# First batch's stage: token tables in four pieces beside the channel tiles, the odd weight sums in the other room, the weight work pinned to the outer rows alone

## The chip, the cores and the metric

The kernel runs on one core of one Trainium2 chip. Five engines work side by side, each through its own instructions in a fixed order: TensorE (PE, with its weight loads as PEld), VectorE (DVE), ScalarE (ACT), GpSimd (POOL) and SyncE (SP), which here only issues transfers. They wait for each other through semaphores. The metric is the device time of one execution in microseconds. The kernel before has a median of 2423.64 us over three runs (2421.47 to 2424.58).

## The reference

The kernel computes one encoder layer for two inputs ("batches") of 1024 tokens by 1024 channels, with the same weights, in float32.

```python
def encoder_layer(x, g_pre, w_in, ...):
    xn = rmsnorm(x, g_pre)
    p = xn @ w_in
    fv, fg, hv, hg, mg = jnp.split(p, ...)
    fz = fv.astype(jnp.float32).reshape(B, L, F_GROUPS, F_GROUP_DIM)
    fz = jnp.fft.fftn(fz, axes=(1, 3), norm="ortho").real
    y_f = (fz * jax.nn.silu(fg)) @ w_fourier_out
    ...
    y_h = (z.astype(dt) * jax.nn.silu(hg)) @ w_hyena_out   # z: two long convolutions
    g_f, g_h = jnp.split(jax.nn.sigmoid(mg + b_merge), 2, axis=-1)
    out = (g_f * y_f + g_h * y_h) @ w_out
    return x + rmsnorm(out, g_post)
```

The change lies in the first 65 us, where the first batch is normalised and multiplied with the part of `w_in` that makes `fv`, and where the token half of the Fourier transform begins.

## The kernel before, in words

Every float32 operand of a matrix product is split into a high and a low part (`split`): ACT rounds the source into the high part (line 170), and DVE or POOL subtracts it from the source to get the low part (line 180). A product is then three matrix multiplications (`mm3`): high by high, high by low, low by high.

The first batch's stage is `first_half`. Its eight tiles of 128 tokens are loaded in two groups: four outer row tiles (0, 7, 1, 6) and four inner ones (2, 5, 3, 4). For each group, `scale_rows` takes the mean square of each row (ACT, line 335), the inverse root of it in a chain of eleven small DVE instructions (`rstd`, lines 241 to 252), and multiplies the rows by it (line 342 on DVE, line 340 on ACT).

Then the channels are passed in four pairs of tiles (`kp` from 0 to 3), first with the outer rows (`h` = 0) and then with the inner rows (`h` = 1). This document numbers these eight steps h0.0 to h0.3 and h1.0 to h1.3. Each step does the following in `two_tiles`:

- TensorE transposes two tiles of 128 channels (line 358), and ACT copies each from PSUM into `xg`, multiplied by `g_pre` (line 359). `xg` has two rooms. Two columns at its end are set by a POOL memset when `h` is 0 (line 353) and by an ACT copy when `h` is 1 (line 351).
- SP stores each tile to `d_x` (line 361).
- The Fourier transform over tokens is folded: `eo` takes the sum and the difference of a token and its mirror image. The sum is made on DVE. The difference is made on DVE when `h` is 0 and on POOL when `h` is 1.
- `eo` is split into `eh` (ACT) and `el` (DVE).
- TensorE multiplies: 24 products `pfv` for a pair of channel tiles, of which 16 read `eh` and 8 read `el`. The first 8 in the order read `eh` alone.

`two_weights` prepares the weights for a pair of channel tiles: the load of `wfv` (line 384, two rooms), the even sums `wes` and odd differences `wos` on DVE, the casts to `we` and `wo` on ACT, and the low parts: `we` on DVE, `wo` on POOL from the second pair on. `wos` has two rooms, `qp0` and `qp1`, taken in turn. The room `qp0` is also that of the scratch `sq` of `hidden(0)`, the sine layer of the filter network, which runs at the same time.

The program is written in loops, and a scheduler in the compiler puts the instructions of every engine in order by its own forecast of their times. `tc.issue_after(i)` tells it to put those instructions of the enclosed part that run on the engine of instruction `i` behind `i`. In the kernel before, `two_weights` and `two_tiles` of all steps but the first stand behind `self.scaled`, the last row scaling on DVE, which from h0.1 on is that of the inner rows. An engine never reorders at run time.

The token tables `seq` (2 MB), the channel tables `chan` and `chx`, the sign table `alt` and the vector `vec` are loaded in `phase_fourier` once `first_half` has been written down: `vec` by SP, the others by POOL. For `seq` and `chan` a tiny POOL copy from `self.rs` (line 631) holds the load back until the inner rows' inverse roots exist. The tables `th`, `wsh` and `bm`, which the main phase uses, are loaded by SP (line 998).

After the stage, `fourier_half` takes the first half's token transform (`pse`, `pso` from `seq`), the channel transform (`pP`, `pQ` from `chan`), and meanwhile the second half's weights and products run. The second batch follows in another form (`norm`, `xtile`), then the main phase.

Of the kernel before, what the change touches and what calls it, by code (L numbers as in the profile page):

```python
# [16 lines left out]
P = 128  # L17
# [143 lines left out]
class K:  # L161
# [167 lines left out]
    def scale_rows(self, h, px, ss, rs):  # L329
# [7 lines left out]
        for j, m in enumerate(self.ROWS[h]):  # L337
            s = rs[:, 4 * h + j:4 * h + j + 1]
            if j % 2 or (h and j):
                nc.scalar.mul(self.xs[m], self.xs[m], s)  # L340
            else:
                self.scaled = nc.vector.tensor_scalar(self.xs[m], self.xs[m], s, None, op0=MUL)

    def two_tiles(self, h, kp, px, fo):
# [4 lines left out]
        xg = px.tile([P, 2, 514], F32, tag="xg", name=f"xg0_{h}{kp}", bufs=2)  # L349
        if h:  # L350
            nc.scalar.copy(xg[:, :, 512:513], fo["r6"][:, ks].unsqueeze(2))
        else:
            nc.gpsimd.memset(xg[:, :, 512:514], 0.0)
# [17 lines left out]
        self.sub("pool" if h else "dve", eo[:, :, 1], fw, bw)  # L371
# [18 lines left out]
    def first_half(self, pw, W, fo, px, pf):  # L390
# [9 lines left out]
        made = None  # L400
        for h in range(2):
# [187 lines left out]
    def phase_fourier(self):  # L589
        tc, nc, a = self.tc, self.nc, self.a  # L590
        with ExitStack() as es:
# [18 lines left out]
            for t in [fo[n] for n in ("x5", "x5t", "xx", "px")] + fo["ex"]:  # L610
                if len(t.shape) > 2:
                    t = t.rearrange("p a b -> p (a b)")
                nc.vector.tensor_scalar(t, self.ident[:, 0:1].to_broadcast(list(t.shape)), 0.0, None, op0=MUL)
            for b in range(NB):
# [3 lines left out]
                if b == 0:  # L618
                    self.hidden(0, px, pf)
                    W = self.open_weights(pw)  # L620
                    made, begun = self.first_half(pw, W, fo, px, pf)
# [5 lines left out]
                for half in ((0, 1), (1, 0))[b]:  # L627
                    if b + half == 0:
                        nc.sync.dma_start(self.vec, a["c_vec"])
                        for t in ("seq", "chan"):  # L630
                            nc.gpsimd.tensor_copy(fo[t][:, 0, 0:1], self.rs[:, 7:8])
                        nc.gpsimd.dma_start(fo["seq"], a["c_seq"])
# [341 lines left out]
    def phase_main(self, nct=8, nb=NB, nf=16):  # L974
        tc, nc, a = self.tc, self.nc, self.a
        with ExitStack() as es:
# [20 lines left out]
            for t, n in ((self.th, "c_th"), (self.wsh, "w_short"), (self.bm, "b_merge")):  # L997
                nc.sync.dma_start(t, a[n])
# [583 lines left out]
```

## Time and profile before

| | us |
|---|---|
| median of three runs | 2423.64 |
| lowest, highest run | 2421.47, 2424.58 |
| time of the profiled execution | 2421.76 |
| its span | 2420.0 |
| PE busy in the span | 2370.0 |
| DVE busy | 1902.7 |
| ACT busy | 1072.7 |
| POOL busy | 511.5 |

The time of the profiled execution is 1.8 us more than its span, and 1.9 us under the median. In the views below, a window row gives for each engine the busy time in that stretch and in brackets the number of instructions, then the granted TensorE clock (1.00 is full), the busy share of the transfer engines and the GB/s. A row of waits names the waiting engine and tile, what ended the wait, the sum, how often, and the longest. A timeline row gives start, duration, engine, line, operation, tiles, and in square brackets the idle time before it with its releaser.

### The profile page before, as it was taken

The page shows a single profiled execution, that of the slowest core. Times are in us where ns is not written, and L with a number is a line of the kernel's source. Part 1 is how long each engine was busy: PE and PEld are TensorE (multiplying, and loading weights), DVE is VectorE, ACT ScalarE, POOL GpSimd, SP SyncE. Part 2 cuts the span into 40 slices and gives each one's busy share as a digit, 9 for nine tenths or more (in the row PEclk, how much of TensorE's full clock was granted, in tenths as well). Part 3 has the DMA queues.
Part 4 walks back from the last instruction along what each step waited for, and adds up shares of the span by engine and source line. Part 5 has one row for each costly group of instructions (what it writes and reads, how often), then busy time and mean ns, then how long its engine had stood idle before and what let it go on. Part 6 is the DMA issues. An engine that isn't in the chain of part 4 may idle for free.

```text
span 2420.0 us, 36378 instructions
## 1 busy us (share of the span) xinstructions
PE 2370.0 (98%) x13000; PEld 2057.5 (85%) x13000; DVE 1902.7 (79%) x3388; ACT 1072.7 (44%) x2037; POOL 511.5 (21%) x521
## 2 busy tenths in 40 slices
PE   5999999999999999999999999999999999999998
PEld 4988888888888888888888888888888888888886
DVE  7776898889749999999889999866555456665677
ACT  6546676767533333333222222332444444444443
POOL 3341222222243334441000000112100111122111
PEclk9999999999999999999999999999999999999999
DMA  7546655555565555546444444445444667786443
GB/s 273 167 147 209 201 182 169 167 176 173 159 204 179 174 168 186 163 153 213 138 132 144 135 138 141 132 138 179 164 162 156 205 211 258 242 269 220 160 158 131
DMA packets 228480, 428.33 MB, mean 177 GB/s; under 512 B 23734, under 2 KB 89592, under 8 KB 227914
## 3 DMA queue, kind: packets, MB, share of 16 engines
q1 hardware_dynamic: 201069, 333.11, 42.9%
q0 software_dynamic: 27008, 92.86, 11.3%
q8 instruction: 102, 1.67, 0.3%
q14 instruction: 80, 0.66, 0.1%
q10 hardware_dynamic: 221, 0.04, 0.0%
HBM read 290.12 MB, written 135.79 MB: 176 GB/s over the span
## 4 chain that ended last, share of the span: by engine, by line
PE 53%; DMA 1%; DVE 1%; issue 1%; ACT 0%; POOL 0%; DVEq 0%; ACTq 0%; POOLq 0%
PE pin L193 18%; PE pg L193 7%; PE pyh L193 7%; PE po L193 6%; PE pyf L193 6%; PE pT L193 4%; PE pX L193 4%; DMA wr<-in_w_fo 1%; PE tph L892 1%; DMA wh<-d_w 0%; DVE b L180 0%; DVE wl L180 0%; DVE t L180 0%; DVE o L176 0%; ACT wh L170 0%
## 5 line engine op out<-in xcount | busy, mean ns | idle before, releaser
L193 PE MATMUL pin<-xh,wh 128*128 128x512 f32 x1472 | 576.6, 392 | 2.4 <-DMA wh<-d_w 1.2
L193 PE MATMUL pin<-xh,wl 128*128 128x512 f32 x1472 | 577.0, 392 | 1.5 <-DMA wr<-in_w_in 1.5
L193 PE MATMUL pin<-xl,wh 128*128 128x512 f32 x1472 | 576.4, 392 | 1.2 <-DVE xl L180 1.2
L180 POOL TENSOR_TENSOR wl<-wr,wh 128x512 fp32r<-128x512 f32 x136 | 255.7, 1880 | 1121.6 <-ACT wh L170 1080.4
L193 PEld LDWEIGHTS pin<-xh,wh 128*128 128x128 f32 x1472 | 277.1, 188 | 55.5 <-DMA wh<-d_w 2.1
L193 PEld LDWEIGHTS pin<-xl,wh 128*128 128x128 f32 x1472 | 277.2, 188 | 53.8 <-DVE xl L180 2.0
L193 PEld LDWEIGHTS pin<-xh,wl 128*128 128x128 f32 x1472 | 277.2, 188 | 53.4 <-POOL wl L180 2.2
L170 ACT CAST wh<-wr 128x512 fp32r<-128x512 f32 x264 | 163.4, 619 | 330.8 <-PE pin L193 102.0
L193 PE MATMUL pX<-bh,cfwd 128*128 128x256 f32 x768 | 162.0, 289 | 0.0
L180 DVE TENSOR_TENSOR wl<-wr,wh 128x512 fp32r<-128x512 f32 x128 | 87.9, 687 | 93.5 <-ACT wh L170 93.4
L180 DVE TENSOR_TENSOR t<-pX,k 128x1024 f32<-128x1024 f32 x128 | 155.4, 1214 | 5.5 <-PE pX L193 3.8
L193 PE MATMUL pyf<-sf,wh 128*128 128x512 f32 x512 | 157.8, 389 | 0.0
L193 PE MATMUL pyh<-sh,wh 128*128 128x512 f32 x512 | 157.4, 389 | 0.0
L193 PE MATMUL pT<-cinv,yh 128*128 128x256 f32 x768 | 145.6, 285 | 0.0
L170 ACT CAST bh<-b 128x512 fp32r<-128x512 f32 x144 | 88.7, 619 | 111.5 <-DVE b L180 76.0
L193 PEld LDWEIGHTS pX<-bh,cfwd 128*128 128x128 f32 x768 | 126.7, 191 | 2.7 <-DVE t L180 0.4
L193 PEld LDWEIGHTS pT<-cinv,yh 128*128 128x128 f32 x768 | 123.2, 190 | 6.6
L170 ACT CAST yh<-y 128x512 fp32r<-128x512 f32 x96 | 59.5, 619 | 138.0 <-DVE y L180 135.5
L193 PEld LDWEIGHTS pyf<-sf,wh 128*128 128x128 f32 x512 | 96.2, 188 | 19.9
L193 PEld LDWEIGHTS pyh<-sh,wh 128*128 128x128 f32 x512 | 96.1, 188 | 19.9
L193 PE MATMUL pT<-cinv,yl 128*128 128x256 f32 x384 | 109.5, 285 | 0.1
L193 PE MATMUL pX<-bl,cfwd 128*128 128x256 f32 x384 | 108.9, 283 | 0.6 <-DVE bl L180 0.6
(372 smaller groups left out, 5318.1 us busy)
## 6 DMA issues: line engine op xcount, KB each, us to landing
k<-d_k SPq DMA_DIRECT2D x128, 512.0 KB, 4.2
wr<-in_w_in SPq DMA_DIRECT2D x136, 256.0 KB, 3.2
d_g<-gt SPq DMA_DIRECT2D x124, 256.0 KB, 2.6
d_k<-kt SPq DMA_DIRECT2D x128, 128.0 KB, 2.2
d_k<-kt SPq DMA_DIRECT2D x64, 256.0 KB, 2.5
wr<-in_w_fo POOLq DMA_DIRECT2D x64, 256.0 KB, 4.1
g<-d_g SPq DMA_DIRECT2D x64, 256.0 KB, 4.2
wr<-in_w_ho POOLq DMA_DIRECT2D x64, 256.0 KB, 3.8
```

The source lines that it names most:

```text
L170: self.rounded = nc.scalar.copy(h, src)
L180: return e.tensor_tensor(out, a, b, op=op)
L193: return self.nc.tensor.matmul(out, lhsT, rhs, start=start, stop=stop, skip_group_check=shared)
L892: nc.tensor.transpose(tp[:, q * P:(q + 1) * P], eo[:, e, q], self.ident)
```

## The change

- `scale_rows`: of the inner rows, the third is scaled on DVE and no longer on ACT. `self.scaled` becomes that instruction.
- `two_tiles`: the end columns are always set by a POOL memset (one column when `h` is 1, beside the ACT copy), which becomes `self.cleared`. The difference in `eo` is always on DVE.
- `two_weights`: the odd differences `wos` take the rooms in the other order, so that the first pair takes `qp1` and not the room of the sine layer's scratch.
- `first_half`: `two_weights` of the second to fourth pair stands behind the outer rows' last DVE scaling alone; `two_tiles` still stands behind the inner rows' one. After each step, POOL issues a part of the tables behind that step's memset: the four pieces of `seq` (even high, even low, odd high, odd low) with steps h0.2 to h1.1, `alt` with h1.0, `chan` and `vec` with h1.2, and `chx`, `th`, `wsh` and `bm` with h1.3.
- The loads in `phase_fourier` and `phase_main` that this replaces, and the two tiny POOL copies, are gone.

```diff
@@ scale_rows
-            if j % 2 or (h and j):
+            if j % 2:
                 nc.scalar.mul(self.xs[m], self.xs[m], s)
             else:
                 self.scaled = nc.vector.tensor_scalar(self.xs[m], self.xs[m], s, None, op0=MUL)
@@ two_tiles
+        self.cleared = nc.gpsimd.memset(xg[:, :, 512 + h:514], 0.0)
         if h:
             nc.scalar.copy(xg[:, :, 512:513], fo["r6"][:, ks].unsqueeze(2))
-        else:
-            nc.gpsimd.memset(xg[:, :, 512:514], 0.0)
...
         self.add("dve", eo[:, :, 0], fw, bw)
-        self.sub("pool" if h else "dve", eo[:, :, 1], fw, bw)
+        self.sub("dve", eo[:, :, 1], fw, bw)
@@ two_weights
-        wo = pf.tile([P, 2, 256], F32, tag=f"qp{kp % 2}", name="wos", bufs=1)
+        wo = pf.tile([P, 2, 256], F32, tag=f"qp{1 - kp % 2}", name="wos", bufs=1)
@@ first_half
-        made = None
+        scaled, made = self.scaled, None
...
             for kp in range(4):
+                if h == 0 and kp:
+                    with tc.issue_after(scaled.ins):
+                        self.two_weights(px, pw, pf, W, kp)
                 with tc.issue_after(self.scaled.ins) if h + kp else ExitStack():
-                    if h == 0 and kp:
-                        self.two_weights(px, pw, pf, W, kp)
                     self.two_tiles(h, kp, px, fo)
+
+                with tc.issue_after(self.cleared.ins):
+                    for t, src in later[4 * h + kp]:
+                        self.nc.gpsimd.dma_start(t, src)
@@ phase_fourier
+            n = 4 * 258
+            seq = [(fo["seq"][:, h, n * e:n * e + n], a["c_seq"][:, h, n * e:n * e + n])
+                   for e in range(2) for h in range(2)]
+            later = [[], [], seq[0:1], seq[1:2], seq[2:3] + [(fo["alt"], a["c_alt"])], seq[3:4],
+                     [(fo["chan"], a["c_chan"]), (self.vec, a["c_vec"])],
+                     [(fo["chx"].rearrange("p a b c -> p (a b c)"), a["c_chx"]), (self.th, a["c_th"]),
+                      (self.wsh, a["w_short"]), (self.bm, a["b_merge"])]]
...
-                    if b + half == 0:
-                        nc.sync.dma_start(self.vec, a["c_vec"])
-                        for t in ("seq", "chan"):
-                            nc.gpsimd.tensor_copy(fo[t][:, 0, 0:1], self.rs[:, 7:8])
-                        nc.gpsimd.dma_start(fo["seq"], a["c_seq"])
-                        nc.gpsimd.dma_start(fo["alt"], a["c_alt"])
-                        nc.gpsimd.dma_start(fo["chan"], a["c_chan"])
-                        nc.gpsimd.dma_start(fo["chx"].rearrange("p a b c -> p (a b c)"), a["c_chx"])
-                    elif b + half != 2:
+                    if b + half not in (0, 2):
@@ phase_main
-            for t, n in ((self.th, "c_th"), (self.wsh, "w_short"), (self.bm, "b_merge")):
-                nc.sync.dma_start(t, a[n])
```

More of the change, by code (lines that the diff above doesn't have):

```diff
@@ L388, in two_weights, with first_half @@
             self.split(*[p[:, 2 * kp:2 * kp + 2] for p in W[i]], r, "pool" if kp and i else "dve", "act")
-    def first_half(self, pw, W, fo, px, pf):
+    def first_half(self, pw, W, fo, px, pf, later):
         tc = self.tc
@@ L620, in phase_fourier @@
                     W = self.open_weights(pw)
-                    made, begun = self.first_half(pw, W, fo, px, pf)
+                    made, begun = self.first_half(pw, W, fo, px, pf, later)
                 else:
```

## The prediction

> **What bounds the kernel now.** I read the page's head, the busy time by stage, TensorE's waits in the changed stage, and then the stage's timeline.
>
> ```profile
> PE 2370.0 (98%) x13000; PEld 2057.5 (85%) x13000; DVE 1902.7 (79%) x3388; ACT 1072.7 (44%) x2037; POOL 511.5 (21%) x521
> 17.90:25.70 7.80, 6.41 (x24) 4.29 (x24) 3.48 (x14) 7.25 (x14) 0.20 (x2) 1.00 0.39 136
> 25.70:39.00 13.30, 11.07 (x73) 10.54 (x72) 11.49 (x18) 11.20 (x19) 5.31 (x7) 0.87 0.93 310
> 39.00:50.00 11.00, 7.26 (x56) 6.48 (x55) 10.28 (x15) 8.12 (x17) 6.68 (x3) 1.00 0.78 263
> 50.00:60.00 10.00, 7.99 (x64) 7.58 (x63) 9.76 (x11) 3.92 (x9) 6.12 (x5) 1.00 0.71 249
> 60.00:70.00 10.00, 10.00 (x86) 9.87 (x85) 3.65 (x11) 3.45 (x10) 3.34 (x5) 1.00 0.04 15
> ```
>
> From 60 us TensorE is full: 86 matmuls in 10 us, 0.116 us each. From 25.7 to 60 it does 193 in 34.3 us, and these would take 22.4 us at that pace. So some 12 us are lost in this stage, and DVE is the busy engine there (9.76 of the last 10 us). Then DVE is nearly idle (3.65 of 10) and TensorE still works: it has piled up work. What ends its waits:
>
> ```profile
> PE pfv L193 <- ACT eh L170: 4.1, 2, 2.2
> PE pfv L193 <- POOL wo L180: 1.8, 2, 1.4
> PE pfv L193 <- DVE el L180: 1.6, 1, 1.6
> ```
>
> ACT's `eh` is itself held up (the waits of ACT), and the groups of DVE and POOL from 18 us show by whom:
>
> ```profile
> ACT eh L170 <- POOL eo L180: 4.7, 3, 2.7
> L180 DVE TENSOR_TENSOR el<-eo,eh 128x1024 fp32r<-128x1024 f32 x8 | 12.4, 1546 | 0.9 <-ACT eh L170 0.8
> L180 DVE TENSOR_TENSOR eo<-xg 128x512 f32<-128x512 f32 x12 | 9.4, 812 | 0.4 <-ACT xg L359 0.2
> L180 DVE TENSOR_TENSOR we<-wes,we 128x520 fp32r<-128x520 f32 x3 | 3.4, 1134 | 0.0
> L180 DVE TENSOR_TENSOR wer<-wfv 128x260 f32<-128x260 f32 x2 | 2.3, 1184 | 0.0
> L180 POOL TENSOR_TENSOR eo<-xg 128x512 f32<-128x512 f32 x4 | 9.5, 2364 | 8.5 <-ACT xg L359 4.7 <-DVE el L180 3.8
> L180 POOL TENSOR_TENSOR wo<-wos,wo 128x512 fp32r<-128x512 f32 x3 | 5.1, 1700 | 0.8 <-ACT wo L170 0.8
> L180 POOL TENSOR_TENSOR wor<-wfv 128x256 f32<-128x256 f32 x2 | 1.9, 960 | 0.0
> ```
>
> POOL needs 2.36 us for a difference for which DVE, alone, needs 0.62 (four in 2.49, below). And DVE slows down beside POOL: the rows below show `el` at 1.21 us alone and 2.10 beside POOL's `wo`. Against the undisturbed 1.22 (`el`), 0.62 (`eo`), 0.69 (`we`) and 0.42 (`wer`), the four DVE groups hold 2.6 + 2.0 + 1.3 + 1.4 = 7.3 us too much, beside 16.5 us of POOL subtraction.
>
> ```profile
> 13.75 0.61 ACT L170 CAST we<-wes 128x520 fp32r<-128x520 f32 x1
> 13.87 0.76 DVE L180 TENSOR_TENSOR wos<-wfv 128x256 f32<-128x256 f32 x2 [1.07 <-ACT hd L270]
> 14.62 0.69 DVE L180 TENSOR_TENSOR we<-wes,we 128x520 fp32r<-128x520 f32 x1
> 22.28 0.17 DVE L241 TENSOR_SCALAR rs_m<-ss 128x4 f32<-128x4 f32 x1 [3.77 <-ACT sq L335]
> 24.61 1.04 ACT L170 CAST eh<-eo 128x1024 fp32r<-128x1024 f32 x1
> 27.02 0.76 DVE L342 TENSOR_SCALAR x<-x,rs 128x1024 f32<-128x1024 f32 x1
> 27.04 3.23 ACT L340 ACTIVATE x<-x,rs 128x1024 f32<-128x1024 f32 x3
> 27.70 0.42 DVE L180 TENSOR_TENSOR wes<-wfv 128x260 f32<-128x260 f32 x1
> 29.05 2.49 DVE L180 TENSOR_TENSOR eo<-xg 128x512 f32<-128x512 f32 x4
> 31.21 1.04 ACT L170 CAST eh<-eo 128x1024 fp32r<-128x1024 f32 x1
> 31.39 1.91 POOL L180 TENSOR_TENSOR wo<-wos,wo 128x512 fp32r<-128x512 f32 x1 [0.85 <-ACT wo L170]
> 32.28 2.10 DVE L180 TENSOR_TENSOR el<-eo,eh 128x1024 fp32r<-128x1024 f32 x1
> 32.30 0.74 PE L193 MATMUL pfv<-we,eh 128*128 128x260 f32 x4 [2.17 <-ACT eh L170]
> 45.53 1.77 DVE L180 TENSOR_TENSOR eo<-xg 128x512 f32<-128x512 f32 x1 [0.16 <-ACT xg L359]
> 57.89 1.21 DVE L180 TENSOR_TENSOR el<-eo,eh 128x1024 fp32r<-128x1024 f32 x1
> 67.57 0.64 PE L193 MATMUL pse<-seq,ee 128*128 128x258 f32 x4
> ```
>
> The last `el` is done at 59.1, and TensorE reaches the end of the first half's products at 67.57. That instant is what the sum below moves. From there on the kernel is TensorE's, which is busy for 98% of the span.
>
> **The change part by part.** Orders are those of the two built programs, durations those of the rows above.
>
> *Odd sums in the other room.* `wos` of the first pair no longer waits for ACT's `hd` (1.07 us). But the chain of the outer rows has `we` in it, which needs ACT's cast (to 14.36 us). So `we` comes at 14.40 and not at 14.62: 0.2 us gained.
>
> *Weight work pinned to the outer rows.* The sums and differences of the second pair, and one more, now stand in DVE's idle 3.77 us before 22.28. But the rest of the third pair's work goes in ahead of the inner rows' scaling: two `wos`, two `wes` (0.34 from start to start) and two `we` (0.69), together 2.7 us. And ACT gets two casts ahead of the transposed tiles of h0.1, which puts `eh` of h0.0 (24.61) back by 0.4 to 1.2 us; that is covered, since TensorE waits later anyway. So the scaling starts at 27.02 + 2.7 - 0.2 = 29.5. With one more scaling on DVE (two, 1.45 us), `eo` of h0.1 starts at 31.0 and not 29.05, is done at 32.2, `eh` at 33.3, and TensorE goes on at 33.3 and not at 32.30. This is a loss. Its upper end: POOL's `wo` of the second and the third pair now run beside `eo` and `el` of h0.0, which by the rows cost DVE 0.9 us (2.10 against 1.21) and 1.15 (1.77 against 0.62). TensorE then goes on at 35.4. ACT's third scaling going to DVE saves ACT 1.07 and costs DVE 0.72; both are in these numbers.
>
> *Differences on DVE.* Four more on DVE cost 4 x 0.62 = 2.5 us and take 9.5 us off POOL. POOL keeps 7.0 us of subtraction, so of the 7.3 us lost by slowing some 7.3 x 7.0 / 16.5 = 3.1 stay, and 4.2 come back. DVE's account: -4.2 + 2.5 + 0.7 (scaling) - 2.0 (six small sums, 0.34 each, in idle time) = -3.0. The last `el` is done at 56.1, or, if the 4.2 do not come back, at 60.3. Behind it stand 16 products, 1.9 us: 62.2 at the latest. This does not set the end, since TensorE's own work does:
>
> *TensorE.* The order has 222 matmuls from the products of h0.1 to the end of the half. They take 222 x 0.116 = 25.8 us. To this come the slower clock behind the wait, 5 x (0.15 + 0.19) = 1.7 us by the rows below, and short waits for PSUM, 0.5 to 1.1 us. From 33.3: 61.3. From 35.4 with the longer waits: 64.0. Against 67.57 that is 6.3 or 3.6 us less; both ends rest on the same two rows, and I take the middle, **5.0 us**. The gain comes mostly from products that no longer pile up: the `wo` products of the inner rows are in step with the others in the new order, while before they came behind the last `el`.
>
> ```profile
> 30.00:35.00 5.00, 2.77 (x16) 2.43 (x15) 4.73 (x6) 4.60 (x10) 2.01 (x2) 0.85 0.92 371
> 35.00:40.00 5.00, 4.12 (x28) 3.88 (x26) 3.50 (x7) 2.40 (x5) 1.54 (x1) 0.81 0.99 319
> 135.00:140.00 5.00, 3.75 (x21) 3.73 (x21) 5.00 (x7) 3.56 (x7) 3.46 (x3) 0.66 0.52 209
> 120.00:140.00 20.00, 15.48 (x115) 14.55 (x114) 19.50 (x30) 14.90 (x25) 11.29 (x11) 0.91 0.84 298
> seq<-in_c_seq POOLq DMA_DIRECT2D x1, 2064.0 KB, 9.7
> 27.76 0.53 POOL L632 DMA_DIRECT2D seq<-in_c_seq  x1
> wfv<-in_w_fv SPq DMA_DIRECT2D x20, 260.0 KB, 3.4
> ```
>
> *Tables in pieces, on POOL.* Costed at nothing. TensorE first reads `seq` behind 160 of the 222 matmuls, about 53 us; its two pieces are issued with h0.2 and h0.3, before 35 us, and the whole table took 9.7 us to land. The odd pieces are needed after 65 us and issued by 46. SP loses four small issues. POOL gains seven issues (0.53 each, 3.7 us) and four tiny memsets, and loses two tiny copies. Behind them on POOL stand the `wo` subtractions and the memsets, and each memset holds an `xg`, so ACT's copy. The tightest is h1.1's: behind the fourth pair's `wo` and a `wor` it comes about 39.5, and its transposes about 42. If that 2.5 us of cover is gone, ACT and then `eo` of h1.1 are late by what is missing; TensorE has h0.3 to do meanwhile.
>
> *Behind the stage.* The second half's weights start when TensorE has read the first half's for the last time, so they move with it. All later work is the same; its order is shuffled up to about the 3,700th matmul. I cost that at nothing, between the bounds of the rivals.
>
> The sum: -5.0 us. The profiled execution took 2421.76, so it would be 2416.8; this execution lies 1.9 under the median of the runs, and against the median of 2423.64 it is **2418.6**.
>
> **The rivals.**
>
> *The inner rows come later still, and the clock drops (0.12).* The third pair's first `wos` is ahead of `eo` of h0.0, and its weights can be asked for only when a room is free, about 19 us; with 3.4 us to land they are there when DVE comes (22.6). If they are 1 us late, all behind is: products from 36.4, after a wait of 6 us. The longer wait can cost more clock: the row from 135 us shows 0.66, 1.7 us lost in 5. Then 36.4 + 25.8 + 1.7 + 1.7 + 1.1 = 66.7, and only 0.9 us are left: 2422.7. [...]
>
> *The shuffled order behind the stage wins (0.22).* TensorE's idle time from 120 to 140 us is 4.5 us, with 1.8 of clock (0.09 x 20). If the new order avoids most of it, it is some 5 us more: 2413.6. For it: nothing but that DVE is full there (19.50 of 20) and could start earlier. Against it: the same tiles in the same form.
>
> *The shuffled order loses: slower (0.18).* The place is the second batch's tiles. There TensorE's order has transposes and first-batch products in turn, and a transpose that stands ahead of its transfer, or of DVE, holds ready products behind it. One more such stretch costs 4.5 + 1.8 = 6.3 us. The gain of 5.0 is used up by it; the kernel is slower by more than 0.2% when 9.9 us are lost. Two more stretches, 12.6 us, give 2431.2. Against it: the tiles, transfers and products are the same, and whatever the stage gains gives DVE an earlier start there.
>
> *The change does not do what it says* would be: POOL is still the one that `eh` waits for, through its memsets. It is in the first rival's range.
>
> **How the numbers follow.** A measurement of this kernel tells about 0.2%, 4.8 us, from no change. The forecast has 0.48, its own range 2415 to 2422, with 0.27 of it below 2418.8. Faster: 0.27 + 0.22 = 0.49. Within: 0.21 + 0.12 = 0.33. Slower: 0.18. The range from 2411 to 2428 takes in the forecast, the first two rivals with their spread (2413.6 less 2.6; 2422.7) and the mild end of the third; what it leaves out is about 0.17 above and 0.03 below.
>
> **What would show it.** Step by step in the changed kernel: `we` of the first pair about 14.4; the products of h0.1 from 33.3 to 35.4, so a longer wait there than 2.17; no POOL `eo` row, and no wait of `eh` for POOL; fewer DVE microseconds in `el`, `eo` and `we` by about 4, except for four more `eo`; the first-half products ending between 61 and 64; no wait for `seq` or `chan`. Wrong would be: products of h0.1 after 36.5, a wait of ACT for a memset, `el` still at over 1.5 us on average, or TensorE's idle time from 75 to 280 us more than 5 us above that of before.

## The result, and the profile after

| | before | changed |
|---|---|---|
| median of six runs on one chip, us | 2424.11 (2421.47 to 2427.22) | 2412.94 (2410.63 to 2416.65) |
| ratio, 95% interval | | 0.9955 (0.9942 to 0.9968) |
| the same kernel in a later comparison, us | 2422.77 | 2414.54 (2412.45 to 2417.91) |
| ratio, 95% interval | | 0.9968 (0.9955 to 0.9980) |
| time of the profiled execution, us | 2421.76 | 2412.46 |
| its span, us | 2420.0 | 2410.7 |

The kernel became faster by 0.45% (0.32% in the second comparison). That is 11 and 8 us; 5.0 were forecast. The time lies in the predicted range (2411 to 2428), under the likeliest case's own (2415 to 2422), and near the rival "the shuffled order behind the stage wins" (2413.6). It lies in the range because the range was made to take in that rival.

The rows by stage, for the same stretches as before:

```profile
17.90:25.70 7.80, 6.07 (x24) 4.44 (x25) 5.57 (x15) 7.42 (x15) 2.29 (x4) 1.00 0.60 190
25.70:39.00 13.30, 9.86 (x70) 9.38 (x68) 13.16 (x25) 10.64 (x19) 6.07 (x7) 1.00 0.75 218
39.00:50.00 11.00, 9.75 (x83) 9.54 (x82) 9.24 (x15) 6.95 (x15) 6.03 (x8) 1.00 0.94 287
50.00:60.00 10.00, 10.00 (x87) 9.87 (x86) 5.06 (x8) 4.30 (x9) 2.24 (x5) 1.00 0.79 239
120.00:140.00 20.00, 17.38 (x134) 16.93 (x133) 19.97 (x33) 12.16 (x20) 13.64 (x11) 0.91 0.69 246
```

From 39 to 60 us TensorE now does 170 matmuls; before it did 120. It is full from 46 us on, not from 60. From 25.7 to 39 it does no more than before (70 against 73), because the products of h0.1 wait longer. TensorE's waits in the stage, and the groups of DVE and POOL from 18 to 60 us:

```profile
PE pfv L193 <- ACT eh L170: 4.2, 2, 2.9
PE tpx L357 <- ACT xg L358: 1.5, 3, 0.5
PE pfv L193 <- DVE el L180: 0.5, 1, 0.5
```

```profile
L180 DVE TENSOR_TENSOR el<-eo,eh 128x1024 fp32r<-128x1024 f32 x8 | 10.5, 1328 | 3.5 <-ACT eh L170 3.4
L180 DVE TENSOR_TENSOR eo<-xg 128x512 f32<-128x512 f32 x16 | 10.2, 684 | 0.3 <-ACT xg L358 0.3
L180 DVE TENSOR_TENSOR we<-wes,we 128x520 fp32r<-128x520 f32 x3 | 2.1, 689 | 0.0
L180 POOL TENSOR_TENSOR wo<-wos,wo 128x512 fp32r<-128x512 f32 x3 | 8.5, 2822 | 3.9 <-ACT wo L170 3.9
```

The wait for POOL's `wo` is gone, and so is POOL's `eo`. DVE's `el` has a mean of 1.33 us (1.55 before), its `eo` 0.68 (0.81). The instants of the stage, in order of time (start, duration, engine; in brackets the idle time before it and its releaser):

```profile
13.87 0.70 DVE L180 TENSOR_TENSOR we<-wes,we 128x520 fp32r<-128x520 f32 x1 [0.99 <-ACT we L170]
30.01 1.42 DVE L342 TENSOR_SCALAR x<-x,rs 128x1024 f32<-128x1024 f32 x2
31.34 2.49 DVE L180 TENSOR_TENSOR eo<-xg 128x512 f32<-128x512 f32 x4
32.66 1.05 ACT L170 CAST eh<-eo 128x1024 fp32r<-128x1024 f32 x1 [0.46 <-DVE eo L180]
33.76 0.74 PE L193 MATMUL pfv<-we,eh 128*128 128x260 f32 x4 [2.93 <-ACT eh L170]
37.12 4.51 POOL L180 TENSOR_TENSOR wo<-wos,wo 128x512 fp32r<-128x512 f32 x1 [1.58 <-ACT wo L170]
43.33 0.19 ACT L352 COPY xg<-r 128x2 f32<-128x2 f32 x1 [3.58 <-DMA d_x<-xg]
43.42 1.04 ACT L170 CAST eh<-eo 128x1024 fp32r<-128x1024 f32 x1
44.52 0.74 PE L193 MATMUL pfv<-we,eh 128*128 128x260 f32 x4 [1.25 <-ACT eh L170]
52.28 0.10 POOL L350 MEMSET xg<- 128x2 f32 x1 [5.46 <-DMA d_x<-xg]
57.35 1.23 DVE L180 TENSOR_TENSOR el<-eo,eh 128x1024 fp32r<-128x1024 f32 x1 [1.02 <-ACT eh L170]
62.35 0.41 PE L193 MATMUL pse<-seq,ee 128*128 128x258 f32 x2
```

The half ends at 62.35; before it was 67.57. ACT and POOL now wait for stores out of `xg` (3.58 and 5.46 us). Behind ACT's wait stands an `eh` whose `eo` DVE had done by 40.48, and TensorE waits 1.25 us for it. At POOL's wait TensorE has work in hand (10.00 us busy from 50 to 60).

Where the 9.2 us up to the last product come from is read off fixed places in TensorE's order, which are the first `pse` behind the half's 192 products ("end of the half"), the first `pin`, the first and the last `pXf` (the filter phase) and the last `po`. Here and below each number is a start or the difference of two starts. "Again" is a second profiled execution of each kernel.

| stretch, us | before | again | changed | again |
|---|---|---|---|---|
| start to end of the half | 67.57 | 67.77 | 62.35 | 62.74 |
| to the first pin | 144.08 | 144.80 | 139.73 | 141.37 |
| to the first pXf | 60.85 | 59.69 | 58.06 | 58.10 |
| to the last pXf | 393.95 | 393.96 | 396.76 | 396.84 |
| to the last po | 1743.20 | 1742.94 | 1743.57 | 1742.21 |

Taken first against first and again against again, 5.0 to 5.2 us come from the stage, 3.4 to 4.4 from the stretch behind it, and 1.6 to 2.8 from the next one. The filter phase takes 2.8 back.

### The profile page after: what moved, and what is told of

It reads as the page before. It is cut to its first block, busy times and chain, and to the rows that moved or that the text cites. A ratio compares the mean times of both kernels' runs of the same rounds, so it can differ in the third digit from the quotient of the medians.

```text
span 2410.7 us, 36396 instructions
## 1 busy us (share of the span) xinstructions
PE 2368.0 (98%) x13000; PEld 2056.8 (85%) x13000; DVE 1903.5 (79%) x3393; ACT 1073.0 (45%) x2038; POOL 509.2 (21%) x526
## 3 DMA queue, kind: packets, MB, share of 16 engines
q0 software_dynamic: 27568, 92.94, 11.2%
## 4 chain that ended last, share of the span: by engine, by line
PE 53%; DVE 0%; DMA 0%; issue 0%; DVEq 0%; ACT 0%; ACTq 0%
PE pin L193 16%; PE pg L193 8%; PE pyh L193 7%; PE pyf L193 7%; PE po L193 6%; PE pT L193 4%; PE pX L193 4%; PE tph L895 1%; DMA wh<-d_w 0%; DVE o L176 0%; DVE xl L180 0%; DVE yc L180 0%; DVE t L180 0%; DVE rs_t L246 0%; DVE rs L247 0%
```

## The experiments

"Undone" takes one part out of the changed kernel; "alone" puts one part into the kernel before. The table at the head of each group holds what was measured: the start of the products of h0.1, the end of the half, the stretch from the first pin to the first pXf (all in us, from one profiled execution), and the median time with its ratio to the kernel before on the same chip (95% interval).

### One part undone

| undone | h0.1 | end | pin to pXf | median | ratio |
|---|---|---|---|---|---|
| nothing (changed kernel) | 33.76 | 62.35 | 58.06 | 2412.94 | 0.9955 |
| differences on DVE | 34.22 | 65.83 | 58.08 | 2418.84 | 0.9981 (0.9972 to 0.9989) |
| the other room | 35.05 | 68.12 | 58.04 | 2418.59 | 0.9984 (0.9975 to 0.9993) |
| the pinning | 32.11 | 64.85 | 63.09 | 2421.57 | 0.9990 (0.9982 to 0.9999) |
| the tables | 38.80 | 68.38 | 62.84 | 2423.39 | 1.0000 (0.9991 to 1.0009) |

**Differences of the inner rows on POOL again.**

```diff
-        self.sub("dve", eo[:, :, 1], fw, bw)
+        self.sub("pool" if h else "dve", eo[:, :, 1], fw, bw)
```

> The changed kernel with one part undone: the four differences of the inner rows are POOL's again. TensorE's order is that of the changed kernel from the 255th matmul on. Theory A (pinning and order of the weights make the stage's gain; TensorE's own work sets its end): the first half's products end at 62.4 to 64.5 us (62.35 in the changed kernel, 67.57 before). Theory B (POOL's slow differences held the stage before): they end at 65.5 to 67.5. Behind the stage: if the extra lead of the changed kernel (5.2 us at the end of the half, 12.4 when the first filter product pXf starts) comes from the new order there, 5 us or more of extra lead stay, since that order is kept, and the whole is 2413 to 2416 us by A, 2416 to 2419 by B; if the extra lead grows out of the stage's lead, it shrinks with it, and the whole is 2414 to 2417 by A and 2420 to 2424 by B.

The end at 65.83 is just inside theory B: this part is worth 3.5 us of the stage. Most of it is one wait. The rows of POOL, DVE and TensorE:

```profile
55.04 3.00 POOL L180 TENSOR_TENSOR eo<-xg 128x512 f32<-128x512 f32 x2
54.59 3.52 DVE L180 TENSOR_TENSOR x<-r,x 128x16 fp32r<-128x16 f32 x1
58.16 2.11 PE L193 MATMUL pfx<-we,x 128*36 128x260 f32 x16 [2.46 <-DVE x L180]
```

A subtraction of 16 columns, which takes DVE 0.18 us in the changed kernel, takes 3.52 here. It ends with POOL's last two differences (58.11 and 58.04), and TensorE waits for it. (Its row begins 0.45 us before that of the two differences; where the overlap starts is not resolved.)

**The odd sums back in the room of the scratch.**

```diff
-        wo = pf.tile(..., tag=f"qp{1 - kp % 2}", name="wos", bufs=1)
+        wo = pf.tile(..., tag=f"qp{kp % 2}", name="wos", bufs=1)
```

> The changed kernel with the odd sums back in the room in which the first pair waits for ACT's hd. TensorE's order differs between the 97th and the 163rd matmul alone. All theories: the first pair's we is 0.2 to 0.6 us later, the first half ends at 62.4 to 63.2 us, and the whole is 2412.5 to 2414 us, no change that can be measured. If the room mattered more than that (the third pair's sums wait for a room that is still read), the end of the half is 64 or later.

The end is past 64, but not for the reason named there (no row of DVE waits for a room). The whole loses 5.8 us in the stage over a part that was priced at 0.2. The order written down for POOL is another one, and its rows show what that costs:

```profile
35.33 3.58 POOL L180 TENSOR_TENSOR wor<-wfv 128x256 f32<-128x256 f32 x1 [5.91 <-DMA wfv<-in_w_fv]
38.85 0.10 POOL L350 MEMSET xg<- 128x4 f32 x1
38.98 3.44 DVE L180 TENSOR_TENSOR eo<-xg 128x512 f32<-128x512 f32 x2 [0.57 <-POOL xg L350]
```

POOL stands for 5.91 us at a `wor` of the second half's weights, whose load has not landed, and then takes 3.58 us for it beside DVE. Behind it on POOL stands the memset of `xg` for h0.3 (38.85; its counterpart in the changed kernel starts at 32.74), and DVE's `eo` waits for that memset. In the changed kernel the two `wor` stand behind the last `wo`, at 41.98 and 44.39, and the first waits 0.35 us.

**The pinning undone.**

```diff
-                if h == 0 and kp:
-                    with tc.issue_after(scaled.ins):
-                        self.two_weights(px, pw, pf, W, kp)
                 with tc.issue_after(self.scaled.ins) if h + kp else ExitStack():
+                    if h == 0 and kp:
+                        self.two_weights(px, pw, pf, W, kp)
                     self.two_tiles(h, kp, px, fo)
```

> The changed kernel with the weight work of the pairs 1 to 3 held behind the latest scaling again, not behind the outer rows' alone. Theory A (the pinned weight work costs a later start of the inner rows but keeps the products in step, and that is most of the gain): the inner rows' scaling starts near 27.0 us, the products of h0.1 near 32.3, yet the first half ends at 65 to 67 us, and the whole is 2416 to 2419. Theory B (the differences on DVE make the gain, and the pinning is a loss of 1 to 3 us): the first half ends at 60.5 to 62 us. TensorE's order behind the stage is a new one here (2,693 places differ up to the 3,716th), so if that order makes the extra lead, it is another number than 7.2 us, of either sign, between the end of the half and the first pXf.

Theory A, in its direction: the scaling starts at 27.01 and the products of h0.1 at 32.11, and yet the half ends 2.5 us later than in the changed kernel (64.85, just under the range). The pinned work delays h0.1 by 1.65 us and still gains. The time, 2421.57, is over theory A's: this kernel has another order behind the stage (below).

**The tables as before.** They stand whole in their old places, and the four small ones on SP.

```diff
-                with tc.issue_after(self.cleared.ins):
-                    for t, src in later[4 * h + kp]:
-                        self.nc.gpsimd.dma_start(t, src)
...
+                    if b + half == 0:
+                        nc.sync.dma_start(self.vec, a["c_vec"])
+                        ...
+                        nc.gpsimd.dma_start(fo["seq"], a["c_seq"])
...
+            for t, n in ((self.th, "c_th"), (self.wsh, "w_short"), (self.bm, "b_merge")):
+                nc.sync.dma_start(t, a[n])
```

> The changed kernel with the tables loaded as before: whole, at their old places on POOL and SP. Theory A (the tables cost and bring nothing in the stage): the first half ends at 62.0 to 62.8 us. Behind it: if the early tables, with POOL's and SP's queues emptied sooner, make the extra lead of 7.2 us between the end of the half and the first pXf, nearly all of it goes, and the whole is 2416 to 2419 us; if the order behind the stage makes it, the number changes with the order, which is a new one here too, and the lead may be anything between 0 and 9; if it grows out of the stage's lead, it stays at 6 to 8 us and the whole is 2412 to 2414.

The whole gain is gone, and 6.0 us of it in the stage, where theory A expected nothing. On DVE the sums of the fourth pair now stand ahead of the inner rows' scaling, TensorE waits 6.49 us for h0.1, and the granted clock is 0.50 from 37.6 to 44.5 us:

```profile
33.45 2.43 DVE L342 TENSOR_SCALAR x<-x,rs 128x1024 f32<-128x1024 f32 x2
38.80 1.23 PE L193 MATMUL pfv<-we,eh 128*128 128x260 f32 x4 [6.49 <-ACT eh L170]
```

This is the outcome of the prediction's first rival: late inner rows, a longer wait, a lower clock. The next group asks which half of the tables part does it.

### The same kernel again, tables alone, the pinning of one pair, the small loads

| kernel | h0.1 | end | pin to pXf | median | ratio |
|---|---|---|---|---|---|
| changed, again | 33.82 | 62.74 | 58.10 | 2414.54 | 0.9968 (0.9955 to 0.9980) |
| tables alone | 31.70 | 68.15 | 58.06 | 2419.36 | 0.9987 (0.9978 to 0.9996) |
| only the second pair pinned | 30.99 | 65.01 | 61.29 | 2416.21 | 0.9976 (0.9967 to 0.9984) |
| small loads on SP again | 36.46 | 67.99 | 58.08 | 2418.90 | 0.9988 (0.9979 to 0.9997) |

> The changed kernel itself, once more, to see what repeats. If stretches between fixed points of TensorE's order belong to the order: the stretch from the first pin to the first pXf is 58.0 to 58.1 us (58.06 in the changed kernel, 58.08 and 58.04 in the two kernels that share its order behind the stage; 60.85 before), the one from the end of the first half to the first pin 139 to 140. If the extra lead was luck of one execution, these differ by 2 us or more. The end of the first half repeats within 1 us of 62.35 (its start hangs on when the rows of x land, which differed by up to 1 us between kernels). Time 2411 to 2415 us.

The end of the half and the stretch from pin to pXf repeat. The stretch from the end of the half to the first pin differs by 1.6 us between two executions of one kernel, outside the 139 to 140 expected. Differences of that size in it are not read below.

**Tables alone**, in the kernel before (the tables part of the diff, nothing else):

```diff
+        self.cleared = nc.gpsimd.memset(xg[:, :, 512 + h:514], 0.0)
...
+                with tc.issue_after(self.cleared.ins):
+                    for t, src in later[4 * h + kp]:
+                        self.nc.gpsimd.dma_start(t, src)
```

> The kernel before with the tables part alone: tables in pieces on POOL inside the stage, the small ones there too instead of on SP, and the clearing of xg for every tile. TensorE's order is that of the changed kernel from the 255th matmul on, in the stage it is nearly that of before. Theory order (the new order behind the stage makes the extra lead): first pin to first pXf is 58.0 to 58.1 us, end of the half to first pin 139 to 144; whatever the stage does, the lead grows by 3 to 7 us behind it, and shrinks by about 2.8 in the filter phase. Theory growth (the extra lead grows out of the stage's lead): it stays at 60.9 us where the stage has no lead. In the stage: if the tables alone bring nothing, the first half ends at 66.5 to 68.5 us and the whole is 2417 to 2421 by theory order, 2422 to 2425 by theory growth. If POOL's and SP's queues were what held the stage, it ends at 62 to 64.

The stage gains nothing by itself (68.15). Yet the kernel is 3.4 us faster, and the stretch from pin to pXf has the 58.06 of the changed kernel, whose order it shares there. That is theory order.

**Only the second pair pinned:**

```diff
-                    with tc.issue_after(scaled.ins):
+                    with tc.issue_after((scaled if kp == 1 else self.scaled).ins):
```

> The changed kernel with only the second pair of weights pinned to the outer rows; pairs 2 and 3 wait for the latest scaling as before. Behind about the 690th matmul its order is that of the kernel before, not that of the changed one (120 places differ behind the 300th). Theory order: first pin to first pXf is 60.8 to 61.0 us as before, and the stage's lead is all the kernel gains: with the first half ending at 61 to 65, 2416 to 2421. Theory growth: the lead grows behind the stage as in the changed kernel, and the whole is 2410 to 2415. In the stage, if the third pair's weight work ahead of the inner rows is a loss (2.7 us in the working of the prediction), the inner rows' scaling starts at 27 to 28 us and the products of h0.1 at 32 to 33; if the pinning of the later pairs keeps the products in step, the end of the half is 64 or later all the same.

The scaling starts at 27.24, which is 2.77 us sooner than in the changed kernel; the working said 2.7 for the third pair. Its half still ends 2.7 us later, as the second theory on the stage had it. The reason is POOL again: the last `wo` starts at 41.02 and takes 5.11 us, and TensorE waits 3.91 us for it. (The row names the memset behind it, which ends 0.04 us later; the product reads `wo` and not `xg`.)

```profile
41.02 5.11 POOL L180 TENSOR_TENSOR wo<-wos,wo 128x512 fp32r<-128x512 f32 x1 [1.45 <-ACT r L362]
46.17 0.58 PE L193 MATMUL pfv<-wo,eh 128*128 128x256 f32 x1 [3.91 <-POOL xg L350]
```

**The small loads on SP again:**

```diff
-                     [(fo["chan"], a["c_chan"]), (self.vec, a["c_vec"])],
-                     [(fo["chx"]..., a["c_chx"]), (self.th, a["c_th"]),
-                      (self.wsh, a["w_short"]), (self.bm, a["b_merge"])]]
+                     [(fo["chan"], a["c_chan"])],
+                     [(fo["chx"]..., a["c_chx"])]]
...
+                        nc.sync.dma_start(self.vec, a["c_vec"])
...
+            for t, n in ((self.th, "c_th"), (self.wsh, "w_short"), (self.bm, "b_merge")):
+                nc.sync.dma_start(t, a[n])
```

> The changed kernel with the four small loads (vec, th, wsh, bm) on SP again, early, as before; seq, alt, chan and chx stay in pieces on POOL. Order behind the stage as in the changed kernel. Theory A (these loads cost nothing): the first half ends at 62 to 63 us, time 2411 to 2415. Theory B (on SP they stand ahead of the weights' loads, which are asked for 1 us later, and take transfer time from the rows of x): 63.5 to 65, time 2413 to 2417. Theory C (they are what makes the kernel with the old tables late): the end is at 66 to 69, and the products of h0.1 wait over 5 us.

Theory C. The end is 67.99 us: with four loads of 0.33 us of SP each back in their place the half ends 5.6 us later. The timeline of SP's queue, DVE, TensorE and POOL:

```profile
20.25 0.38 SPq L360 DMA_DIRECT2D d_x<-xg  x1
20.74 0.90 SPq L383 DMA_DIRECT2D wfv<-in_w_fv  x2
31.03 0.42 DVE L180 TENSOR_TENSOR wos<-wfv 128x256 f32<-128x256 f32 x1 [1.53 <-DMA wfv<-in_w_fv]
32.71 1.42 DVE L342 TENSOR_SCALAR x<-x,rs 128x1024 f32<-128x1024 f32 x2
36.46 1.23 PE L193 MATMUL pfv<-we,eh 128*128 128x260 f32 x4 [5.88 <-ACT eh L170]
35.33 4.99 POOL L180 TENSOR_TENSOR wor<-wfv 128x256 f32<-128x256 f32 x1 [6.24 <-DMA wfv<-in_w_fv]
```

The corresponding requests of the changed kernel:

```profile
18.45 0.33 SPq L383 DMA_DIRECT2D wfv<-in_w_fv  x1
20.30 0.38 SPq L360 DMA_DIRECT2D d_x<-xg  x1
```

The time of the requests alone does not explain this. The second pair's first load is asked for at 12.76 us here; in the changed kernel it was 11.69 in one execution and 12.45 in the other, and both end by 62.74. What differs is the order that is written down, in three queues. On SP the third pair's first load stands behind the first store to `d_x` (20.74), and not ahead of it (18.45). On DVE the sums of the fourth pair's first tile now stand ahead of the inner rows' scaling too, and wait 1.53 us for their load. On POOL a `wor` that waits 6.24 us stands ahead of the memset and the last `wo`, as in the kernel with the old room. The scaling starts 2.7 us later, the products of h0.1 start at 36.46 behind a wait of 5.88 us, and the granted clock is 0.50 from 34.7 to 41.6 us. TensorE is busy for 5.1 us of these, so about 2.5 of the 5.6 us are clock (an estimate: half of the 5.1). Late requests in an unchanged order were not tried.

### The kernel before again, two parts alone, and wo on DVE

| kernel | h0.1 | end | pin to pXf | median | ratio |
|---|---|---|---|---|---|
| before, again | 32.60 | 67.77 | 59.69 | one run | |
| differences on DVE alone | 32.81 | 65.41 | 59.88 | 2420.08 | 0.9994 (0.9985 to 1.0002) |
| pinning and room alone | 37.51 | 69.82 | 64.16 | 2425.85 | 1.0019 (1.0010 to 1.0028) |
| changed, wo on DVE | 35.62 | 64.59 | 60.89 | 2418.90 | 0.9988 (0.9979 to 0.9997) |

> The kernel before once more, for its profile alone: what of its stretches repeats. If the stretch from the end of the first half to the first pin (144.08 us; 139.1 to 141.4 in seven of the nine other kernels) was an execution's luck, it is 139 to 142 now, and the changed kernel's extra lead there is no effect of the change; if it belongs to the kernel, it is 143.5 to 144.5 again. First half's end 67 to 68.5, first pin to first pXf 60.8 to 61.0.

The stretch from the end of the half to the first pin is 144.80: it repeats in the kernel before, against 139.73 and 141.37 in the changed one. Kernels that share the changed one's order there have 139.08 to 143.48, though, so this stretch alone shows little. From pin to pXf it missed: 59.69 against 60.85, so this stretch varies by 1.2 us in that order.

**Differences on DVE alone** (the one line of the first experiment, in the kernel before).

> The kernel before with one part alone: the four differences of the inner rows on DVE. The order behind the stage is nearly that of before (92 places differ behind the 300th). Theory A (each part brings its share of the stage's gain: 3.5 us were lost when this one was undone): the first half ends at 63.5 to 65 us, time 2418 to 2421. Theory B (only the parts together keep the weights, POOL's queue and the products in step): it ends at 66.5 to 68, time 2421 to 2424.

The end at 65.41 lies between the theories, and the time in theory A's range; 2.2 us of the stage. The kernel keeps the old order behind the stage, and the whole gains 2.4 us, about what the stage gave; the interval takes in no gain at all.

**Pinning and room alone** (both edits, in the kernel before).

> The kernel before with the pinning of the weight work and the other room alone; tables, small loads, scaling and differences as before. The small loads stand on SP ahead of the weights here, as in the changed kernel with these loads on SP again, whose products of h0.1 waited 5.9 us until 36.5 and whose half ended at 68.0. Theory C (pinned weight work needs its weights early; with the small loads on SP ahead of them they land late and the inner rows' scaling stands behind them): products of h0.1 at 35.5 to 39 after a wait of over 4.5 us, a clock under 0.9 behind it, the first half ends at 67.5 to 70, time 2422 to 2426, no gain or a loss. Theory A (pinning is a gain by itself): products of h0.1 by 34.5, end at 63 to 66, time 2417 to 2421.

Theory C: slower than before. The scaling starts at 32.84, TensorE waits 5.81 us, and the granted clock is 0.50 from 34.1 to 40.9 us:

```profile
37.51 1.24 PE L193 MATMUL pfv<-we,eh 128*128 128x260 f32 x4 [5.81 <-ACT eh L170]
```

**All wo on DVE**, in the changed kernel:

```diff
-            self.split(..., r, "pool" if kp and i else "dve", "act")
+            self.split(..., r, "dve", "act")
```

> The changed kernel with the differences wo of the weight pairs 1 to 3 on DVE instead of POOL (they take 0.68 us on DVE; on POOL 1.58, 2.37 and 4.51 in the changed kernel). Behind the stage its order is nearly that of before. If POOL's slow wo, with the clearing of xg behind it, still costs the changed kernel something: the first half ends at 60.5 to 62 us. If DVE is what the stage has least of: 2 us more on DVE, the products of h0.1 1 to 2 us later, the half ends at 63 to 65. First pin to first pXf 60.8 to 61.3, as in the kernels with that order. Time 2412 to 2419.

The end is 2.2 us later, as the second case has it, but the rows do not show DVE short of time: ahead of the scaling it stands idle. The sums of the fourth pair's first tile again stand there and wait 2.26 us for their load, and the inverse root's next small instruction, whose input was done at 28.33, starts behind them at 31.28. TensorE waits 6.16 us for h0.1, and the granted clock is 0.50 from 32.7 to 39.6 us:

```profile
30.60 0.43 DVE L180 TENSOR_TENSOR wos<-wfv 128x256 f32<-128x256 f32 x1 [2.26 <-DMA wfv<-in_w_fv]
35.62 1.23 PE L193 MATMUL pfv<-we,eh 128*128 128x260 f32 x4 [6.16 <-ACT eh L170]
```

No kernel of these beats the changed one.

### What they say together

*The stage.* Against the mean of the two executions of before (67.67), the differences alone give 2.3 us, tables alone lose 0.5, pinning and room alone lose 2.2. Their sum is a loss of 0.4; together (with the third scaling on DVE, which was not tried by itself) they gain 4.9 to 5.3. So it is the combination that gains. Taking the room or the four small loads away costs more than the whole gain, since in each case weight work that is not ready stands at the head of DVE's or POOL's queue.

*Behind the stage.* Three orders occur there. The table takes the gain of the medians and subtracts the stage's lead against 67.67:

| order behind the stage | kernel: gain, stage's lead, rest (us) |
|---|---|
| the changed kernel's | changed 11.2, 5.3, **5.9**; again 8.2, 4.9, **3.3**; differences undone 4.6, 1.8, **2.8**; room undone 4.8, -0.5, **5.3**; tables alone 3.4, -0.5, **3.9**; small loads on SP 3.9, -0.3, **4.2** |
| that of before, nearly | differences alone 2.4, 2.3, **0.1**; wo on DVE 3.6, 3.1, **0.5**; one pair pinned 6.6, 2.7, **3.9** |
| other orders | pinning undone 1.9, 2.8, **-1.0**; tables undone 0.0, -0.7, **0.8**; pinning and room alone -3.4, -2.2, **-1.2** |

The rest is 2.8 to 5.9 in all six results with the changed kernel's order, whatever the stage does, and under 1 in five of the other six. One kernel (one pair pinned) does not fit. The table sets medians against a lead from one execution, though, and that kernel's profiled execution took 2420.59 us, 4.4 above its median. Within single executions (the time against 2421.52, the mean of the two of before, less the same lead) the rest is 0.8 to 6.2 in the six with the changed order and -3.6 to 0.3 in the six others, with -1.7 for that kernel.

TensorE's idle time says the same more directly. From the end of the half to the first pXf it is 5.5 to 7.3 us in the six executions with the changed order, and 9.5 to 12.0 in the eight others. The first row is of the kernel before, the second of the changed one:

```profile
67.57:272.50 204.93, 193.45 (x1397) 180.14 (x1396) 156.69 (x351) 112.93 (x233) 67.30 (x75) 0.99 0.57 187
62.35:260.14 197.79, 192.28 (x1392) 179.99 (x1391) 154.38 (x354) 111.18 (x235) 69.92 (x76) 0.99 0.59 192
```

The filter phase gives some of it back: in the changed kernel TensorE is idle there for 1.6 us, before not at all. So the order behind the stage is worth some 3 to 6 us, 4 on average. It comes with the tables part, by itself too. The tables in pieces are not enough for it, since three kernels that have them in another order (pinning undone, one pair pinned, wo on DVE) have 10.5 us or more of idle. Which rows of the new order make it is not seen. The order alone, with the same stage, was not tried.

## Why the prediction was right or wrong

- **Odd sums in the other room**: right in direction in this kernel, wrong as a price. `we` came at 13.87, not 14.40; `hd` itself was 0.5 us sooner, the rows of `x` having landed earlier (the last at 16.54 us, before at 17.44). In the kernel before, POOL asks for `alt` and `chx` at 2.5 and 3.1 us, among the loads of `x`; whether their absence is the reason was not tried alone, and with the pinning undone `x` landed at 17.48 without them. The part was costed at 0.2 us. Undone, it costs 5.8 us of the stage, because the other engines' orders change with it.
- **Weight work pinned to the outer rows**: right in its instants, by two misses that cancel. Scaling at 30.01 (29.5 predicted), `eo` at 31.34 (31.0), `eh` done 33.71 (33.3), products of h0.1 at 33.76 (33.3 to 35.4). But the chain for the inner rows' inverse root began at 21.35 and not 22.28. And the slowing by POOL, which the working had only at its upper end, did come, in another place: `el` and the four `eo` were undisturbed (1.21 and 2.49 us), while two instructions of that chain took 2.2 us too long beside POOL's `wo` (rows in the last section). One of these is in the 2.77 us of the third pair, too; its work by itself is nearer to 2.0 than to 2.7 (four sums at 0.34 and one `we` at 0.61 from start to start).
- **Differences on DVE**: right in direction, the last step ahead of the end mis-sized. The last `el` is done at 58.6 (56.1, or 60.3 without the return). The four groups were to give back 4.2 of 7.3 us; by the same reckoning (busy time less the undisturbed one) `el` now holds 0.7 us too much, `eo` 0.3, `we` and `wer` next to nothing, so some 6 came back. But `eh` came late for the last two `el` (2.21 and 1.02 us); ahead of the first of these ACT waits 2.15 us for a store out of `xg`. That the last `el` does not set the end held in the changed kernel; undone, POOL's last differences do set it (2.46 us of wait).
- **TensorE**: right in its sum, in part by luck. The half ends at 62.35, between 61.3 and 64.0; -5.2 and -5.0 us in two executions, -5.0 taken. The 222 matmuls are there, but the other terms are not those of the sum. The slower clock, 1.7 us, was needed in one of the two executions: the clock was 1.00 throughout in the first, and 0.50 from 33.6 to 37.0 us in the second. In the first, the matmuls took 26.8 us (25.8 predicted) and TensorE was idle for 1.8 us: 1.25 behind ACT's wait for a store, which was costed at nothing, and 0.5 behind DVE's `el`. The short waits for PSUM, 0.5 to 1.1 us in the sum, were an estimate; none stands in these rows.

```profile
33.76:62.35 28.59, 26.82 (x222) 26.25 (x223) 20.66 (x35) 17.11 (x36) 11.30 (x16) 1.00 0.88 268
```

- **Tables in pieces, on POOL**: the step that failed. It was costed at nothing ("SP loses four small issues"). With these four on SP again the half ends 5.6 us later: the rows show SP, DVE and POOL in other orders, in which weight work that is not ready holds the scaling and the memset. That is the outcome of the first rival, and close to its numbers (products "from 36.4", measured 36.46; the end 66.7 there, measured 67.99), but not its mechanism: the rival had the third pair's weights late because of the rooms of `wfv`, while the long waits were the fourth pair's (1.53 us) and that of POOL's `wor` (6.24 us). That the instant agrees is luck.
- **Behind the stage**: the term of the sum that was mis-sized. Costed at nothing; it gave 3.3 to 5.9 us by the medians. That is the second rival, with its mechanism (less idle TensorE) and about its size (5 us). Its place, 120 to 140 us, is seen only in part: TensorE is idle there for 2.6 and 3.9 us in the changed kernel, 4.5 and 4.7 before, but for 3.9 to 5.3 in the four other kernels with the same order. It got 0.22 because nothing but DVE's fullness spoke for it; the tables alone, with no lead in the stage, show 3.4 us.
- **The other rivals.** The shuffled order did not lose here, but does elsewhere: with pinning and room alone the kernel is slower by 0.19%, 2.2 us of it in the stage and 1.2 behind. In the changed kernel no row of DVE, ACT or TensorE waits for a memset; with the room undone an `eo` does, for 0.57 us.
- **Of the signs named as wrong**, one came in another form: ACT waited 3.58 us for a store out of `xg`, for which a memset of the same tile waits as well, and this cost TensorE 1.25 us. The other signs did not come: `el` stayed under 1.5 us, and TensorE's idle time fell.

## What to carry to other kernels

Where several engines run written-out orders, a moved load also moves what the scheduler writes behind it. Look up in the built program what stands at the head of each queue, and what it waits for: four requests of 0.33 us, put back on SP, came with 5.6 us, because other weight work then stood ahead of the next rows' scaling and of the memset. Parts of such a change cannot be priced one by one and added; undo each one, and run it alone, before it is called free. When a sum comes out right, check its terms too: here the stage's did so by misses that cancelled. And when a change shuffles the order behind it, read the time of fixed places further on: here two fifths to a half of the gain was made there.

## What the runs showed of the hardware

**The clock after a wait.** The granted clock fell to 0.50 after a wait of 2.17 us in the kernel before, and stayed at 1.00 after one of 2.93 us in the changed one. In each of the fourteen traces its changes lie a whole number of 3.41 us apart, and the drops in this stage last one or two such lengths (3.41 us in the kernel before, 6.9 with the tables undone). So cut the time into windows of this length, at the trace's own changes. In the kernel before, the wait lies in one window, TensorE is busy for 1.18 of the 3.41 us, and the next window has 0.50. In the changed kernel it falls on two windows, with 2.00 and 1.90 us busy, and the clock stays full. In the second execution of the changed kernel a wait of 3.59 us fills a whole window (0.06 us busy), and the next has 0.50. The two windows of each, in this order:

```profile
30.08:33.49 3.41, 1.18 (x8) 0.92 (x8) 3.27 (x5) 3.41 (x7) 2.01 (x2) 1.00 0.87 355
33.49:36.90 3.41, 3.41 (x17) 3.41 (x18) 3.28 (x4) 2.84 (x6) 0.00 (x0) 0.50 0.96 328
```

```profile
28.83:32.25 3.42, 2.00 (x17) 1.76 (x16) 3.31 (x9) 2.19 (x2) 0.00 (x0) 1.00 0.81 278
32.25:35.66 3.41, 1.90 (x16) 1.86 (x16) 3.41 (x8) 3.00 (x4) 1.82 (x5) 1.00 0.32 48
```

```profile
30.17:33.58 3.41, 0.06 (x1) 0.00 (x0) 3.41 (x6) 2.95 (x3) 0.43 (x2) 1.00 0.44 153
33.59:37.00 3.41, 3.18 (x15) 3.18 (x16) 3.41 (x7) 3.41 (x9) 1.37 (x4) 0.50 0.68 184
```

Over all fourteen traces, from the first record of the clock (26.66 us in the kernel before, 28.83 in the changed one) up to 2400 us, the 17 windows at full clock in which TensorE was idle for 2.0 us or more were all followed by 0.50. Of the 21 with 1.6 to 2.0 us idle, 8 were; of the 9,653 with less, one was (1.37 us). So in these traces the idle time within a window tells nearly all the drops apart, with the edge between 1.6 and 2.0 us of the 3.41; the length of the wait alone does not. By this count it was luck that the changed kernel's first execution kept its clock: its 2.93 us fell on two windows, with 1.41 and 1.51 us idle.

**DVE and POOL side by side.** With the differences undone, the 16-column subtraction above took DVE 3.52 us (0.18 in the changed kernel) and ended with POOL's, at 58.11 and 58.04. In the changed kernel the same shows in two small instructions of the inverse root, whose like took 0.15 to 0.17 us elsewhere in that trace. They took 1.24 and 1.25 us, and ended within 0.03 us of POOL's `wo` (24.62 and 24.59, 28.70 and 28.68). With all `wo` on DVE none of these took over 0.17 us.

```profile
23.01 1.58 POOL L180 TENSOR_TENSOR wo<-wos,wo 128x512 fp32r<-128x512 f32 x1 [1.54 <-ACT wo L170]
23.38 1.24 DVE L251 TENSOR_TENSOR rs_t<-rs_t,rs_m 128x4 f32<-128x4 f32 x1
26.31 2.37 POOL L180 TENSOR_TENSOR wo<-wos,wo 128x512 fp32r<-128x512 f32 x1 [0.75 <-ACT wo L170]
27.45 1.25 DVE L251 TENSOR_TENSOR rs_t<-rs_t,rs_m 128x4 f32<-128x4 f32 x1
```

The other way round, POOL's third `wo` in the changed kernel took 4.51 us, from 37.12 to 41.63, while DVE went through its instructions back to back at their undisturbed pace (two `eo` in 1.29). DVE fell idle at 40.48 (its next instruction starts at 41.93), and POOL was done 1.15 us later:

```profile
39.19 1.29 DVE L180 TENSOR_TENSOR eo<-xg 128x512 f32<-128x512 f32 x2
```

In the kernel before, POOL's `wo` took 1.46 to 1.91 us. What held the engines back is not shown. For the kernel these rows mean that the prediction's price, DVE's time lost in proportion to POOL's, was too simple: both engines lost time. DVE spent 1.24 and 1.25 us on instructions of 4 columns and 3.52 us on one of 16, and POOL spent 4.51 us on a `wo` beside a busy DVE, with its next instruction at 41.98 behind it.
